# A column roll in HBM: every long row piece cut in two, one half on each of the two hardware DMA rings

## The chip, the cores and the metric

The kernel runs on 1 core of one Trainium2 chip. The metric is device time in microseconds (us). A run whose time is over 1.5% above the fastest of the same kernel is called slow and is not used for a comparison. Runs come in jobs: the kernels of one job run on the same chip, each beside runs of the kernel before.

## The reference

```python
x = np.random.randn(8192, 8192).astype(np.float32); shift = 100
return np.roll(x, shift, axis=1)
```

That is 268.4 MB to read and as much to write, with no arithmetic.

## The kernel before

Columns 128 and up (`a = 128`) are copied from HBM to HBM, one piece of 8064 floats (32,256 bytes) per row, in 16 big DMAs that alternate between SP's and ACT's ring. (SP and ACT are SyncE and ScalarE, here only as issuers; a ring is the queue in which an issuer's copies wait for the 16 DMA engines.) The rows `64c + 4e + j` of one `e` are one of 16 equal shares, meant for one DMA engine each. The first 128 columns, where the wrap is, go through SBUF on GpSimd's ring.

```python
xm = x.rearrange("(c e j) w -> j e c w", e=16, j=4)
om = out.rearrange("(c e j) w -> j e c w", e=16, j=4)
depth = n_rows // 64 // 4
for c in range(4):
    for j in range(4):
        if a < n_cols:
            cs = slice(c * depth, (c + 1) * depth)
            engines[j % 2].dma_start(out=om[j, :, cs, a:], in_=xm[j, :, cs, g:n_cols - s])
# ... cut: the head, columns 0 to 127, GpSimd's DMAs through SBUF tiles t and h
```

## Time and profile before

| | before |
|---|---|
| timed runs, median (lowest to highest) | 828.66 us (828.28 to 829.5, 6 runs) |
| the profiled run, span | 817.17 us, 815.4 us |
| moved by the DMA engines | 272.63 MB, of which 8.39 by GpSimd's ring |
| HBM traffic over the span, read and written | 658 GB/s |

The kernel is a stream of copies: what counts is how fast the 16 DMA engines move bytes.

### The profile page before, as it was taken

To read this page: it belongs to the slowest core of one execution; us is meant where nothing else is said; L and a number is where in the kernel's file an instruction comes from. 1 tells how busy PE (TensorE), PEld (TensorE's weight loads), DVE (VectorE), ACT (ScalarE), POOL (GpSimd) and SP (SyncE) were. 2 spreads that over 40 slices of the span, in tenths; PEclk is the share of its full clock that TensorE was granted. 3 is DMA by queue.
4 is the path that set the end of the run, shared out by engine and by line. 5 is a ranking of instruction groups with operands and counts; after the bars stand their busy time and mean duration, and the time that the engine had idled before them with its cause. 6 is when DMAs were issued, how large, how long until landed. Compare 5 with 4: busy or idle time off the path is not lost. (4 is left out here: it accounts for less than half of the span.)

```text
span 815.4 us, 93 instructions
## 1 busy us (share of the span) xinstructions
DVE 3.7 (0%) x4; POOL 16.1 (2%) x22
## 2 busy tenths in 40 slices
DVE  0000000000000000000000000000000000000000
POOL 3000001000010000000000000000000000000000
DMA  9999999999999999999999999999999999999996
GB/s 310 341 328 347 330 349 335 337 340 346 338 337 346 338 348 348 347 333 345 340 344 337 349 326 335 334 329 334 335 329 331 329 335 334 332 331 332 329 334 250
DMA packets 10784, 272.63 MB, mean 334 GB/s; under 512 B 544, under 2 KB 544, under 8 KB 2592
## 3 DMA queue, kind: packets, MB, share of 16 engines
q10 hardware_dynamic: 4224, 132.12, 47.0%
q1 hardware_dynamic: 4224, 132.12, 46.9%
q0 software_dynamic: 2336, 8.39, 4.5%
HBM read 268.44 MB, written 268.44 MB: 658 GB/s over the span
## 5 line engine op out<-in xcount | busy, mean ns | idle before, releaser
L76 POOL DMA_DIRECT2D out_dram<-h x8 | 6.9, 954 | 170.1 <-DMA h<-in_x_dram 144.1
L67 POOL DMA_DIRECT2D t<-in_x_dram x6 | 5.4, 910 | 0.8 <-PEq L107 0.8
L69 DVE COPY h<-t 128x2400 f32<-128x2400 f32 x2 | 2.8, 1410 | 208.5 <-DMA t<-in_x_dram 208.5
L71 POOL DMA_DIRECT2D h<-in_x_dram x2 | 1.8, 883 | 28.6 <-DMA t<-in_x_dram 28.6
L68 POOL DMA_DIRECT2D h<-in_x_dram x2 | 1.8, 882 | 27.0 <-DMA t<-in_x_dram 27.0
L72 DVE COPY h<-t 128x672 f32<-128x672 f32 x2 | 1.0, 503 | 0.0
L93 POOL MEMSET const-float32-0.0<- 128x1 f32 x1 | 0.1, 99 | 0.2 <-issue 0.2
L93 POOL MEMSET const-bfloat16-1.0<- 128x1 bf16 x1 | 0.1, 103 | 0.0
L93 POOL MEMSET const-float32-1.0<- 128x1 f32 x1 | 0.1, 99 | 0.0
L93 POOL MEMSET const-uint8-127<- 128x1 uint8 x1 | 0.1, 99 | 0.0
## 6 DMA issues: line engine op xcount, KB each, us to landing
out_dram<-in_x_dram SPq DMA_DIRECT2D x8, 16128.0 KB, 401.3
out_dram<-in_x_dram ACTq DMA_DIRECT2D x8, 16128.0 KB, 400.5
out_dram<-h POOLq DMA_DIRECT2D x8, 512.0 KB, 182.5
t<-in_x_dram POOLq DMA_DIRECT2D x6, 512.0 KB, 118.2
h<-in_x_dram POOLq DMA_DIRECT2D x2, 400.0 KB, 151.3
h<-in_x_dram POOLq DMA_DIRECT2D x2, 112.0 KB, 146.1
```

The lines of the kernel that those rows point to most:

```text
L67: nc.gpsimd.dma_start(out=t[:, q - 1], in_=lead)
L68: nc.gpsimd.dma_start(out=h[:, Q - 1, :, :s], in_=xt[k, Q - 1, :, :, n_cols - s:])
L69: nc.vector.tensor_copy(h[:, :Q - 1, :, :s], t[:, :, :, :s])
L71: nc.gpsimd.dma_start(out=h[:, 0, :, s:], in_=xt[k, 0, :, :, :g])
L72: nc.vector.tensor_copy(h[:, 1:, :, s:], t[:, :, :, s:])
L76: nc.gpsimd.dma_start(out=ot[k, q, :, :, :a], in_=h[:, q])
L93: nc = _bacc.Bacc("TRN2", target_bir_lowering=False, num_devices=1)
```

## The change

The intent is to keep both rings in the same row: SP copies the first half of each long piece, ACT the second.

```diff
+    mid = (a + n_cols) // 2 // 128 * 128
     for c in range(4):
         for j in range(4):
-            if a < n_cols:
-                cs = slice(c * depth, (c + 1) * depth)
-                engines[j % 2].dma_start(out=om[j, :, cs, a:], in_=xm[j, :, cs, g:n_cols - s])
+            cs = slice(c * depth, (c + 1) * depth)
+            for q, (lo, hi) in enumerate(((a, mid), (mid, n_cols))):
+                if lo < hi:
+                    engines[q].dma_start(out=om[j, :, cs, lo:hi], in_=xm[j, :, cs, lo - s:hi - s])
```

## The prediction

> **What bounds the kernel now.** I read the page's busy table and slices first, then the DMA queues, then the chain, then SP's own waits, and last the DMA view cut to stretches.
>
> ```profile
> span 815.4 us, 93 instructions
> DVE 3.7 (0%) x4; POOL 16.1 (2%) x22
> DMA  9999999999999999999999999999999999999996
> GB/s 310 341 328 347 330 349 335 337 340 346 338 337 346 338 348 348 347 333 345 340 344 337 349 326 335 334 329 334 335 329 331 329 335 334 332 331 332 329 334 250
> ```
>
> No compute engine matters: VectorE works 3.7 us, GpSimd 16.1 us. The 16 DMA engines are busy in every slice but the last. The job is a copy, and the copy never pauses.
>
> ```profile
> q10 hardware_dynamic: 4224, 132.12, 47.0%
> q1 hardware_dynamic: 4224, 132.12, 46.9%
> q0 software_dynamic: 2336, 8.39, 4.5%
> HBM read 268.44 MB, written 268.44 MB: 658 GB/s over the span
> ```
>
> Columns: packets, megabytes, share of 16 engines' span. q1 and q10 are the rings of SP and ACT, q0 is GpSimd's. Each hardware ring has 4096 data packets of 32,256 bytes (one row piece of 8064 floats; 132.12 MB / 4096) and 128 small ones for the semaphores. The HBM line counts both directions, since the big copies go from HBM to HBM.
>
> The chain of waits is of little help here: it puts 24% down to "another core or an unknown queue" and stops at 242.8 us, where GpSimd has issued its last store. SP's queue shows what comes after:
>
> ```profile
> SPq L107 <- DMA out_dram<-in_x_dram: 317.3, 4, 100.4
> SPq L37 <- DMA out_dram<-in_x_dram: 47.6, 4, 16.7
> ```
>
> After issuing everything (the last issue starts at 415.2 us and takes 81.6), SP only waits for the four copies still in flight. So the end is set by the rate of the big copies, not by issue.
>
> Busy DMA engines can be at their own peak or be slowed by what they talk to. Two readings say the second. First, in the trace's packet records a 32,256-byte packet takes at least 1192 ns, which for 16 engines would be 16 x 32,256 / 1192 = 433 GB/s; the mean is 1494 ns, and only 24% are under 1250 ns. In the thinning end (from 802 us; 12 engines in flight at 807 us, 3 at 813) all 88 big packets that start take about 1194 ns. An engine is at its own speed as soon as fewer compete. Second, the DMA view by stretches:
>
> ```profile
> q1 hardware_dynamic: 1228, 38.58, 44.0%
> q10 hardware_dynamic: 1207, 37.90, 43.9%
> q0 software_dynamic: 1196, 4.24, 11.2%
> ...
> q1 hardware_dynamic: 1591, 49.74, 50.3%
> q10 hardware_dynamic: 1594, 49.84, 49.0%
> ```
>
> The first three are 0 to 240 us, the last two 480 to 780 us. A ring copy touches HBM twice, a GpSimd transfer once (its other side is SBUF). HBM traffic is therefore 2 x (38.58 + 37.90) + 4.24 = 157.2 MB in 240 us, 655 GB/s, and later 2 x 99.58 = 199.2 MB in 300 us, 664 GB/s; the stretch between, worked the same way, gives 668. The moved bytes fall from 336 to 332 GB/s between these stretches although the mix changes, and HBM traffic stays at about 664. **The bound is a ceiling on HBM traffic**: 536.9 MB / 664 GB/s = 808.6 us, and the remaining 6.8 us of the span are the start and the thinning end.
>
> **What the Trainium skill says.** "DMA: Bandwidth & Descriptors", section "Issuing engines are not separate DMA queues": copies from SP, ACT and GpSimd run on the same 16 engines and interleave. Its section "Queues, rings and completion order" says that each engine takes turns between the rings at packet granularity. The trace agrees: in the first 240 us the three rings pass 1228, 1207 and 1196 packets, one each in turn. "HBM Reference", section "Specifications (TRN2)", gives about 716 GB/s for the HBM that two cores share; with one core running I read 664, or 93% of that, so little is left to gain. "DMA: Bandwidth & Descriptors", section "How a descriptor splits into AXI transactions", says that a read must start from a 256-byte boundary and the bytes before the start are fetched for nothing. No view shows such bytes; the HBM line counts only the useful ones.
>
> **The change, part by part.**
> Bytes: the same 264.24 MB over the two rings. With 128 columns kept for the head part and the middle at column 4096, SP's half is 3968 floats (15,872 bytes) and ACT's 4096 floats (16,384 bytes). SP carries 130.0 MB, ACT 134.2 MB. HBM traffic: unchanged, 0 us.
>
> Issues: 16 per ring for 8, each for 16 engines x 32 pieces. The shortest issues in the trace take 0.61 to 0.67 us, so 8 more cost about 5 us per queue. They lie beside the copies: from the fifth on, an issue waits for the copy four before it on the same ring, then sits in a full ring for most of a copy's time (81.6 to 98.8 us), with three copies queued ahead of it. After the change a copy lasts half as long, about 50 us, and three queued copies still cover 150 us of work. On the path: 0 us.
>
> Packets: 8192 per ring for 4096, so 8192 more over 16 engines, 512 each. The fixed cost of a packet, from the fastest records of two sizes (4400 bytes in 172 ns, 32,256 in 1193 ns; estimate): the slope is 1021 ns / 27,856 bytes, which leaves 172 - 161 = 11 ns. 512 x 11 ns = 5.6 us of engine time. But an engine spends 1494 - 1193 = 300 ns of each packet waiting for HBM now, and 22 ns of fixed cost instead of 11 fits into that. Only in the last 10 us, where engines run at their own speed, does it show: about 8 packets x 11 ns = 0.1 us.
>
> Read alignment: source pieces start at column 28, 112 bytes past a 256-byte boundary; the new second piece starts at column 3996, which is again 112 bytes past one. Fetched for nothing, if HBM pays for it as the skill says: 8192 x 112 bytes = 0.92 MB, 0.17% of 536.9 MB, **+1.4 us** (estimate). The writes start on boundaries in both kernels.
>
> Turns: GpSimd gets one turn in three as before, but the other two are now half as long. Three turns took about 4 KB + 2 x 32 KB and now take 4 KB + 2 x 16 KB. Its stores, which land by about 463 us now, should land near 250 us. Nothing waits for them at the end: 0 us.
>
> Sum: 828.8 + 1.4 + 0.1 = about 830 us (the unprofiled median; the profiled run, at 817.2 us, should go to about 818).
>
> **The rivals.**
> (1) The address pattern lowers or raises the HBM ceiling. Before, SP and ACT were on neighbouring rows, so that an engine had 64 KB of neighbouring addresses open at once; now it is both halves of one row, 32 KB, and then on by 64 rows, 2 MiB. If channels are shared less evenly by that, the ceiling falls; the skill's "DMA: Bandwidth & Descriptors", section "Latency and other measured facts", reports copies falling from 207 to 164 GB/s at row pitches of 512 KiB and 2 MiB. Against it: 64 rows are also the step of each ring now, and the kernel still reaches 664 GB/s; the 16 engines stay 128 KiB apart. If it came, 3 to 8%, 855 to 895 us. The other sign is as open: two halves of one row could hit open memory pages more often, but from 664 to 716 GB/s is the most, at best 829 x 664/716 = 769 us; I would expect 800 to 815.
> (2) Each packet pays a latency that the mean of 1494 ns hides. If the 300 ns over the minimum were per packet and not per byte, 512 more packets per engine would cost 154 us, some 980 us. Against it: a quarter of the packets show no such excess, and in the thinning end none does. I give it 2%.
> (3) The rings get out of step: ACT has 3% more bytes. If rings were served by bytes, SP would be done early and ACT would finish alone, with perhaps 4.2 MB left at 332 GB/s or less, within the same total bytes; at worst +5 us if one ring alone drives engines less well. Against it: turns go by packets, and both have 8192.
> (4) The end becomes more even, since a last packet is 0.6 us instead of 1.2: -0.6 us.
>
> **Range and chances.** The main case, bytes and ceiling unchanged, lies between 824 and 835 us and gets 84%. Within 2% is 812 to 845. Rival 1 gets about 7% in each direction, a little more is added for slower by rival 2. I predict 830 us, 8 times in 10 between 818 and 842, with faster 0.07, same 0.84, slower 0.09.
>
> **What the changed profile would show.** The queue lines: 8320 packets on each hardware ring (8192 + 128), 130.0 and 134.2 MB. The DMA row at nines throughout. From the DMA view after GpSimd's ring is empty: 332 GB/s moved, so 664 GB/s of HBM traffic; another figure there is rival 1. Packet records: means near 735 and 760 ns for the halves, half of 1494; if the mean is 850 or more, rival 2. Software transfers over by about 250 us. SP's last waits about 50 us each instead of 100. The prediction is wrong if the rate late in the run differs from 332 GB/s by more than 2%, or if a ring runs empty and the DMA row shows less than nine before the last slice.

## The result, and the profile after

| | before | after |
|---|---|---|
| median (lowest to highest) | 828.66 us (828.28 to 829.5, 6 runs) | 837.16 us (833.53 to 839.59, 6 runs) |
| ratio, 95% interval | | 1.0100 (1.0073 to 1.0126) |

Ratios are the mean time of one kernel's fast runs over that of the other's of the same rounds, so not quite the ratio of the medians quoted. The verdict is "same" at 2%: 1% slower, clear of the noise, and inside the range of 818 to 842.

The page of the changed kernel (busy tenths and GB/s in 40 slices; then ring, packets, megabytes, share of 16 engines' span):

```profile
span 836.3 us, 109 instructions
...
DMA  8999999999999999999999999999999999999993
GB/s 304 335 339 335 340 331 354 336 352 345 343 337 328 324 329 324 330 326 331 332 325 327 332 326 324 328 327 328 332 326 325 329 329 326 328 323 331 328 325 147
...
q10 hardware_dynamic: 8448, 134.22, 47.6%
q1 hardware_dynamic: 8448, 130.02, 46.3%
q0 software_dynamic: 2336, 8.39, 3.8%
HBM read 268.44 MB, written 268.44 MB: 642 GB/s over the span
```

Bytes and busy engines are as before; the last slice moves 147 GB/s where it moved 250, and from the twenty-fourth slice on, when GpSimd's transfers are done in both kernels, the slices lie near 327 where they lay near 332. Each ring has 8192 data packets and 256 small ones. GpSimd's transfers are now over at 251 us, and the faster slices end there, with the twelfth.

SP's own waits (time in total, number, longest):

```profile
SPq L110 <- DMA out_dram<-in_x_dram: 155.8, 8, 47.0
SPq L40 <- DMA out_dram<-in_x_dram: 139.9, 12, 50.1
```

The longest of the last waits (the first line) is 47.0 us where it was 100.4, and there are twice as many, as copies of half the size should give. The waits between issues (the second line) grew from 47.6 to 139.9 us in all. Still no ring ran empty: the DMA row is at nine between the first slice and the last, and in the packet records the two rings move their last data 2.4 us apart.

By the late rate I mean what moved from 480 to 780 us, after GpSimd's ring is done and before the end thins out; HBM traffic is twice that, since a copy from HBM to HBM reads and writes each byte. Set side by side, the two first traces say that late HBM traffic fell from 664 to 655 GB/s, 1.4%, and would have that as the cause. The experiments indicate that most of this gap comes from somewhere else.

### The profile page after: what moved, and what is told of

Its sections match the earlier page's. It is cut to its first block, busy times and chain, and to the rows that moved or that the text cites. A ratio compares the mean times of both kernels' runs of the same rounds, so it can differ in the third digit from the quotient of the medians.

```text
span 836.3 us, 109 instructions
## 1 busy us (share of the span) xinstructions
DVE 3.7 (0%) x4; POOL 16.1 (2%) x22
## 3 DMA queue, kind: packets, MB, share of 16 engines
q10 hardware_dynamic: 8448, 134.22, 47.6%
q1 hardware_dynamic: 8448, 130.02, 46.3%
```

## The experiments

Theories at the start: **P**, more packets cost rate; **A**, two rings inside one row make a worse address pattern; a third, that the new read boundary costs. Later came **placement**: that the first two traces are not of like jobs.

### Job 1: the change again, its arrangement varied, its packets doubled

The kernel before took 828.80 us in this job (11 runs).

**after_again**: the changed kernel, unaltered.

> The changed kernel unaltered, for its own scatter and a second trace. First trace: 327 GB/s moved between 480 and 780 us (654 GB/s of HBM traffic, 664 before), and one engine about 8 us behind the median at the end. If both are properties of the kernel, the ratio is again 1.007 to 1.013, the late rate 326 to 328, and the last 20 us again show one to three engines working alone. If the straggler is chance, the late rate repeats and the end does not.

Measured: 831.66 us, ratio 1.0041 (1.0017 to 1.0065), under the 1.007 to 1.013 expected. The late rate repeated, 2 x (50.02 + 48.36) MB in 300 us, 656 GB/s of HBM traffic. The end was less extreme, so its length is partly chance.

**halves_own_row**: both halves of a row on one ring, rows alternating as before.

```diff
-                    engines[q].dma_start(...)
+                    engines[j % 2].dma_start(...)
```

> The same half pieces, but each row's two halves both on one ring, rows alternating between the rings as in the kernel before. Theory P (the number of packets costs): late rate stays at 327 GB/s, ratio near 1.010. Theory A (two rings inside one row is a worse address pattern): late rate returns to 332, ratio 1.000 to 1.003.

Measured: 842.52 us, ratio 1.0161 (1.0140 to 1.0183). Putting each ring back in its own rows did not bring the rate back: by 780 us it had moved 258.05 MB, after_again 258.12. That is against theory A. It is slower than the change because of its end, with packets of the same sizes and as many DMAs, so the arrangement of the rows over the rings does matter there; its DMA view from 800 to 840 us:

```profile
DMA  9798888868778678677443322132232221110000
GB/s 360 279 377 311 328 311 311 328 246 328 311 311 360 295 328 344 295 328 311 213 197 147 131 115 115 82 131 98 98 131 98 98 115 82 82 49 33 0 0 0
```

One column is 1 us. From the twentieth column on, the 16 engines together move 213 GB/s, then around 100 and less: for some 17 us only a few engines still have work.

**halves_shifted**: SP and ACT as in the change, but two rows apart.

```diff
+                jj = (j + 2 * q) % 4
-                    engines[q].dma_start(out=om[j, ...], in_=xm[j, ...])
+                    engines[q].dma_start(out=om[jj, ...], in_=xm[jj, ...])
```

> First halves on SP, second halves on ACT as in the changed kernel, but ACT works two rows of the group of four away, so that the two rings are never in the same row. Theory A: late rate back to 332 GB/s, ratio 1.000 to 1.003. Theory P: 327 and 1.010.

Measured: four fast runs between 836.64 and 846.41 us, ratio 1.0161 (1.0122 to 1.0200), two slow ones at 853. The time is not what theory A expected (1.000 to 1.003). The trace is of a slow run, so I compare nothing in it, and whether its rate or its end took the time is not shown.

**quarters**: four pieces per row, two on each ring.

```diff
-            for q, (lo, hi) in enumerate(((a, mid), (mid, n_cols))):
+            cuts = [a, 2176, mid, 6144, n_cols]
+            for q in range(4): lo, hi = cuts[q], cuts[q + 1]
-                    engines[q].dma_start(...)
+                engines[q // 2].dma_start(...)
```

> Four pieces per row, the first two on SP, the last two on ACT: 16,384 packets a ring. Theory P: the loss of 1.4% per 8192 packets more than doubles, since three times as many packets are added: late rate 315 to 320 GB/s, ratio 1.03 to 1.045. Theory A: as the changed kernel or less, since both rings are in one row again: 327 and 1.010. If only the 256-byte read boundary costs, 0.17% for each added cut: ratio about 1.005 over the whole.

Measured: 865.06 us, ratio 1.0456 (1.0428 to 1.0484), slower. The direction is theory P's; the late rate, 2 x (49.22 + 47.75) MB in 300 us = 646 GB/s of HBM traffic or 323 moved, is not as low as expected (315 to 320), and the other part is again the end:

```profile
DMA  3321121122111111111111111100000000000000
GB/s 130 140 85 84 74 85 84 74 85 86 64 63 42 64 53 53 53 53 53 53 53 53 53 53 54 54 21 33 22 11 0 0 0 0 0 0 0 0 0 0
```

This is 840 to 870 us in steps of 0.75 us. An engine alone moves about 27 GB/s (16,384 bytes in 608 ns, the fastest of the changed kernel's packet records), so 53 GB/s is two engines, for 9 us.

### Job 2: both kernels with aligned reads, and fewer, larger packets

The kernel before took 818.91 us here (11 runs), 1.2% less than in job 1.

**before_again**: the kernel before, unaltered.

> The kernel before unaltered, for a second trace: its first trace was at 817 us, its timed runs at 826 to 831, so that trace may be of a lucky execution. If the ceiling of 664 GB/s of HBM traffic is the kernel's, the late rate is again 332 GB/s moved and the 11 us are in the thinning end. If the first chip was merely quicker, the late rate is near 327 and nothing of the changed kernel's loss is in the rate.

Measured: 820.45 us, ratio 1.0005 (0.9986 to 1.0025), span 814.7 us. The late stretch, 480 to 780 us:

```profile
q1 hardware_dynamic: 1598, 50.00, 50.5%
q10 hardware_dynamic: 1602, 50.13, 49.2%
```

That is 667 GB/s of HBM traffic. So the first trace of before (817 us, 664 GB/s) was no lucky execution: it fits a job like this one, where before takes 819 us, and not the job of the timed runs at 829 us that it was set beside. Whether the 829 us jobs are slower in rate or at their end was left to job 3.

**whole_aligned**: before, its source moved so that every read starts on a 256-byte boundary. Its output is wrong, which doesn't matter for the time.

```diff
-in_=xm[j, :, cs, g:n_cols - s]
+in_=xm[j, :, cs, :n_cols - a]
```

> The kernel before with the source of the big copies moved back by 28 columns so that every read starts on a 256-byte boundary (result wrong on purpose: the bulk is shifted by 128). If the cut's cost is the misaligned start of its read, this is a little faster than before: ratio 0.998, late rate 332.5. If alignment is of no account: 1.000.

Measured: 820.62 us, ratio 1.0018 (1.0003 to 1.0032). Aligned reads gain nothing here.

**halves_aligned**: the change with the same move. Its output is wrong, which doesn't matter for the time.

```diff
-in_=xm[j, :, cs, lo - s:hi - s]
+in_=xm[j, :, cs, lo - a:hi - a]
```

> The changed kernel with the same move (wrong on purpose), so that both halves read and write from 256-byte boundaries. Alignment theory: the loss is gone, ratio to before 0.998 to 1.001, late rate 332. Packet theory: late rate 327 as in the changed kernel, ratio 1.004 to 1.010.

Measured: 822.20 us, ratio to before 1.0033 (1.0012 to 1.0053); 1.0033 / 1.0018 = 1.0015 over whole_aligned. In the late stretch it ran at 2 x (50.43 + 48.93) / 300 us = 662 GB/s, whole_aligned at 2 x (49.90 + 49.96) / 300 us = 666. The rate loss is there without any misaligned boundary, so alignment isn't its cause. The ratio lies between the two expectations; in the traces the end of the halves was the more even of the two.

**row_pairs**: two rows in one packet of 65,024 bytes, the head stores of odd rows dropped (wrong).

```diff
-    xm = x.rearrange("(c e j) w -> j e c w", e=16, j=4)
+    xm = x.rearrange("(c e j b) w -> j e c (b w)", e=16, j=2, b=2)
...  (out alike; 8 x 2 DMAs over c and j instead of 4 x 4)
-        for q in range(Q):
+        for q in range(0, Q, 2):
```

> The other direction: two whole rows in one packet of 65,024 bytes (the head columns of odd rows are copied along, wrong on purpose, and their own head stores dropped; HBM traffic within 0.4% of before). Packet theory: half as many packets give back about half of what the cut cost, late rate 333 to 335 GB/s, ratio 0.992 to 0.997. If row order or rings were the cause instead: 332 and 1.000 to 1.004.

Measured: 822.07 us, ratio 1.0036 (1.0014 to 1.0058), which is about its 0.4% of extra traffic. Its late HBM traffic, 2 x (49.48 + 49.35) + 1.83 MB (GpSimd's ring is still at work) in 300 us, is 665 GB/s, no higher than before_again's 667. Half as many packets gave nothing back, so theory P in its simple form (each packet saved is time saved) fails above 32 KB. Another reading stays untested: the change and the quarters have two and four times as many DMAs, the row pairs as many as before, so a cost of each DMA and not of each packet would fit all three. The small packets that end each DMA take 9 ns each, in all 0.15 us more per engine after the change; that alone is too little. No kernel that computes the right result beats the kernel before.

### Job 3: both kernels in one job, with and without the head

The kernel before took 829.66 us (11 runs).

**before_3** and **after_3**: both unaltered, so that two traces can be compared at last.

> The kernel before again, in one job with the changed kernel so that both traces come from the same placement: the timed runs of before lay at 829 us in two jobs and at 819 us in the third, and every trace of before so far is of the quick kind. If the late rate moves with the job and not with the kernel, then in a job where this takes 829 us its late HBM traffic is 655 to 658 GB/s, like the changed kernel's, and in a job where it takes 819 us it is 664 to 667.

> The changed kernel in the same job. Rate theory (the cut lowers the HBM ceiling by 1.4%): its late HBM traffic is 9 GB/s under before_3's, ratio 1.010 to 1.014. Placement theory (the 664 to 655 was two jobs, not two kernels): at most 4 GB/s under, ratio 1.002 to 1.010, the remainder in the first 120 us and in the thinning end.

Measured: before_3 828.81 us, ratio 0.9995 (0.9977 to 1.0013); after_3 833.14 us, ratio 1.0057 (1.0026 to 1.0088). The late stretch of before_3:

```profile
q1 hardware_dynamic: 1581, 49.45, 50.5%
q10 hardware_dynamic: 1580, 49.42, 49.4%
```

and of after_3:

```profile
q10 hardware_dynamic: 3143, 49.96, 50.1%
q1 hardware_dynamic: 3141, 48.35, 49.7%
```

Doubled and divided by 300 us these are 659 and 655 GB/s. The kernel before itself loses 8 GB/s from one job to another; within one job the change costs 4. **As far as job 3 stands for the job of the result, more than half of the 664 to 655 was placement, not the kernel.** What differs between such jobs I do not know: the first and the second had the same chip number and differed.

Next, the DMA view from the start to 780 us, before_3 and then after_3. By then GpSimd's ring is done in both, so the megabytes compare like with like:

```profile
DMA packets 10344, 259.47 MB, mean 333 GB/s; under 512 B 512, under 2 KB 512, under 8 KB 2560
```

```profile
DMA packets 18298, 258.12 MB, mean 331 GB/s; under 512 B 765, under 2 KB 765, under 8 KB 2813
```

and from 780 to 840 us (1.5 us a column), before_3:

```profile
DMA  9899999989899898999698868741100000000000
GB/s 366 323 344 280 387 323 323 344 301 366 280 366 301 280 344 323 387 301 366 237 409 280 301 258 344 344 194 65 43 0 0 0 0 0 0 0 0 0 0 0
```

after_3:

```profile
DMA  8998999998998999999998998987631110000000
GB/s 280 355 344 268 355 333 333 344 322 290 323 366 301 366 280 334 344 312 312 365 323 301 354 323 312 367 281 292 261 141 65 43 43 22 22 0 0 0 0 0
```

Two losses can be read apart here. Until 780 us after_3 has moved 1.35 MB less, which at its 328 GB/s is 4.1 us. (The view counts a packet whole at its start; shared out over their duration, the packets give 1.28 MB, 3.9 us.) And its end is longer: before_3 falls from 344 to 0 in about 4 us, after_3 spends its last columns at 65, 43, 43, 22 and 22 GB/s. In the packet records the last 3.6 us of transfers are one packet at a time, of either ring, of 592 or 611 ns, each starting as the last one ends. I read that as one engine alone, at its full speed, that simply has more left than the others. The spans differ by 833.7 - 824.8 = 8.9 us, so the end accounts for 4.8. These two traces overstate the usual difference: before_3's is its quickest run (826.59 us), after_3's is over its median (835.53 us); the ratio of 1.0057 is 4.7 us.

**whole_no_head** and **halves_no_head**: both kernels without GpSimd's part (columns 0 to 127 stay unwritten).

```diff
-    if a == 0:
+    if a >= 0:
         return
```

> The kernel before without GpSimd's head transfers (the first 128 columns stay unwritten, wrong on purpose): the pure cost of the two rings. 528.5 MB of HBM traffic at the late rate: ratio to before 0.984 to 0.990.

> The changed kernel without the head transfers. If the loss of the change comes from the head transfers now crowding into the first 250 us, this equals whole_no_head within 0.1%. If it comes from the halves themselves, it is above whole_no_head by as much as after_3 is above before_3.

Measured: 810.47 us, ratio 0.9770 (0.9751 to 0.9789), faster, and below the range I expected; 819.25 us (the median of six, one of them slow at 830.78), ratio of the fast runs 0.9857 (0.9821 to 0.9893). Between them 0.9857 / 0.9770 = 1.0089. Without any head transfer the halves still cost about as much, so GpSimd's transfers crowding into the first 250 us are not the cause. The end of whole_no_head, 780 to 820 us, and then of halves_no_head:

```profile
DMA  8939979969969587847878825550000000000000
GB/s 323 419 129 484 323 290 323 355 226 419 355 226 419 226 323 323 355 194 323 387 323 355 355 129 226 226 226 32 0 0 0 0 0 0 0 0 0 0 0 0
```

```profile
DMA  9999999899998999898998897863111100000000
GB/s 339 290 371 306 338 356 354 274 340 338 324 323 306 339 355 353 308 322 306 324 338 290 356 323 291 326 262 146 81 48 65 49 16 32 33 16 0 0 0 0
```

The whole pieces end at 226 GB/s, 8 engines at once, and stop; the halves trail off over 9 us.

### The two losses over the pairs of one job

Moved by 780 us, and what the rest took, from the DMA views and the spans. "Steady" is the difference in megabytes over the late rate of the halves (328, 328 and 331 GB/s); "end" is the rest of the difference in span.

| pair | moved by 780 us, MB | span, us | difference, us | steady | end |
|---|---|---|---|---|---|
| before_3, after_3 | 259.47, 258.12 | 824.8, 833.7 | 8.9 | 4.1 | 4.8 |
| whole_no_head, halves_no_head | 255.95, 255.00 | 809.4, 817.2 | 7.8 | 2.9 | 4.9 |
| whole_aligned, halves_aligned | 262.73, 260.63 | 817.9, 821.5 | 3.6 | 6.3 | -2.7 |

Fewer bytes by 780 us appear in all three, but "steady" says more than all of them show. In the pair without the head the two kernels move the same in the late stretch, 98.38 and 98.36 MB; their 0.95 MB were lost before 480 us. And whole_no_head's late traffic, 656 GB/s, lies 3 under before_3's 659, so the 4 GB/s between before_3 and after_3, one trace each, is hardly more than traces of whole pieces differ in one job. What repeats well is the amount of the halves: they had moved 258.01 (first trace), 258.12, 258.12 and, on their own rows, 258.05 MB by 780 us, in three jobs where before took 829 us. The quarters had moved 253.67 MB, 5.80 MB under before_3 (of another job), which at their 323 GB/s is 18.0 us for three added packets per row, 6.0 each; under after_again, of their own job, it is 4.45 MB, 13.8 us for two, 6.9 each. The end loss is there in two pairs and absent in the third; it is what makes the changed kernel's runs scatter, as far as the traces go.

## Why the prediction was right or wrong

The verdict and the range were right, and so, within 1%, was the main argument, that a copy bound by a ceiling keeps its time when its bytes stay. The point, 830, missed 837.16 us by 0.9%; in the two later jobs the change took 831.66 and 833.14 us. Part of this is luck. 837.16 lies above the main case of 824 to 835 us and inside the range only by the room kept for rivals that did not come. The sum had 1.5 us of loss, 1.4 of them for a cause that the aligned runs do not confirm; measured were 8.5 us by the medians, and 2.9 and 3.5 in the later jobs.

- **Bytes, issues and rings: right, but for two counts.** 130.02 and 134.22 MB, no ring empty. Each ring had 8448 packets where 8320 were expected: the small packets go with the DMAs (16 for each), so they doubled too, from 128 to 256. SP's last waits were at most 47.0 us, but 155.8 over 8, so 19 in the mean.
- **Turns: right.** GpSimd's transfers were over by about 250 us (251, 250 and 249 us in three traces; 462 to 467 before). They cost nothing at the end; the pair without the head shows that they are not the loss either.
- **Packets: this is the step that failed.** The prediction put the fixed cost at 11 ns a packet, 5.6 us of engine time, and called it hidden: "22 ns of fixed cost instead of 11 fits into that". The runs show a deficit by 780 us that is worth 2.9 to 6.3 us in three pairs, and 6.0 to 6.9 us per added packet in the quarters. That is the size of the 5.6 us unhidden. The fixed cost itself was sized well, though from packets of two kinds of transfer: in the thinning ends a packet of 32,256 bytes takes 1194 ns and its halves 592 + 611, 9 ns more, or 4.6 us over 512 packets. That this cost, no longer hidden, is the mechanism is only argued. Against it stand the row pairs, which with half the packets gained nothing, and the late stretch without the head, where the halves lose nothing; a cost of each DMA would do as well.
- **Read alignment: not confirmed.** The 1.4 us were charged to misaligned reads. Aligning all reads of the whole pieces gave 1.0018, no gain, and the halves lose rate when aligned too.
- **Rival 4, a more even end: the sign was wrong.** I expected -0.6 us from smaller last packets. In these traces the length of the end is set by how far one or a few engines lag, not by the size of the last packet: 4.8 and 4.9 us longer in two pairs, 2.7 shorter in one. Why an engine falls behind more often with halves is open.
- **Rival 1, the address pattern: not seen in the rate.** Neither the kernel with each ring in its own rows nor the one with the rings two rows apart is quicker than the change; both are slower, at 1.016, the first by its end alone. Rivals 2 and 3: the packet means were 756 and 777 ns, where 735 and 760 were expected and rival 2 asked for 850, and both rings end within 2.4 us of each other.
- **The profiled run "should go to about 818": wrong, with the right mechanism absent.** I took the 11 us between profile and timed runs for the profiler's and scaled. Profiled runs are ordinary timed ones (the changed kernel's profiled run is the 838.12 us among its six). The first trace of before, with its time and its rate, fits the 819 us job and not the runs it stood beside. For the same reason the expected late rate of 332 GB/s was that of an 819 us job; in the job of the result it would, going by before_3, have been about 330 for before, and was 327 for the change, within the 2% that the prediction allowed.

## What to carry to other kernels

This copy was bound by a shared transfer ceiling, and cutting its packets in two without changing the bytes cost little but not nothing, 0.4 to 1.0%. The cost can sit in two places: fewer bytes moved by a late moment (in three pairs of three) and a less even finish of the 16 engines (in two of three). Read the two apart by comparing the bytes moved up to a fixed late moment and the time the remainder took. And before explaining a difference of 1% between two traces, make sure that both come from the same job: here more than half of the apparent loss of late rate was there between two jobs of the unchanged kernel.

## What the Trainium skill lacked or had wrong

- "DMA: Bandwidth & Descriptors", section "Specifications", gives 512 bytes and more as enough for line rate. In these HBM-to-HBM copies the size of the pieces still goes with 1 or 2% far above that (packets and DMAs changed together; one trace each): late HBM traffic of 659 GB/s with packets of 32,256 bytes, 655 with about 16 KB and 646 with about 8 KB (jobs in which before took 829 us), and nothing gained with 65,024 bytes (ratio 1.0036 at 0.4% more traffic).
- "DMA: Bandwidth & Descriptors", section "Latency and other measured facts", has DMA engines 7 and 15 usually slower than the others, and guesses at GpSimd's descriptor rings. It lacks how long the end of a common copy gets by unequal engines, and that this is so without GpSimd too: the quarters spent 9 us with two engines at work, after_3 3.6 us with one, and halves_no_head, in which GpSimd issues no transfer, trailed off over 9 us. The records don't say which engines lag.
- No page that I read says that the HBM rate of an unchanged kernel can differ between jobs: late traffic of 667 and 659 GB/s, medians of 818.9 and 829.7 us.
- "DMA: Bandwidth & Descriptors", section "How a descriptor splits into AXI transactions", tells of bytes fetched for nothing ahead of an unaligned start. For pieces of 32 KB no cost of it was seen (aligned reads: ratio 1.0018).
